# Query norms of a decoder layer moved from the gate stage to the mixer; memory norm moved into the second half of u

## The chip, the cores and the metric

The kernel runs on one core of a Trainium2 chip, in float32. The metric is the time of one execution on the device, in microseconds (us); three runs of the kernel before took 2217.03, 2217.82 and 2221.04 us, median 2217.82. A measurement is read together with the profile of one more execution.

TensorE does the matrix products, VectorE (DVE) and ScalarE (ACT) the elementwise work, GpSimd (POOL) a little of it, and SyncE (SP) issues the transfers. Float32 products are made from two-part numbers: each operand is split into a rounded part `hi` and a rest `lo`, and a product is three matmuls (hi hi, hi lo, lo hi). Every operand therefore costs one copy on ScalarE (the `hi`) and one subtract on VectorE (the `lo`) before TensorE can use it.

## The reference, cut to what matters

One layer: a half-step feed-forward block, a mixer with three branches, an output projection and a second feed-forward block. The change touches the combined projection and branches A and C.

```python
h = rmsnorm(x, mix_norm)                      # 1024 tokens x 1024 features
z = h @ w_in                                  # [u | v | c_q | c_kv | k_rope | q_mem | gate_A | gate_B | gate_C]
u, v = gelu(z_u), gelu(z_v)
y_a = u * (tril(W_s) layernorm(v) + b)        # over chunks of 128 tokens, 8 groups
y_b = latent attention of c_q, c_kv, k_rope   # untouched here
q  = rmsnorm(q_mem per head, mem_q_norm)      # 4 heads of 128
kv = rmsnorm(mem, mem_norm) @ mem_w_kv        # 256 memory tokens
y_c = softmax(q rmsnorm(k)^T / sqrt(128)) v
merged = sum_i sigmoid(gate_i + b_gate_i) * (y_i @ W_branch_i)
x = x + merged @ w_out
```

`rmsnorm(x, g)` is `x * rsqrt(mean(x*x) + 1e-6) * g`. The root of a query head is a number per token and head; it can be applied after the scores, and the kernel does so: queries go into the scores with their gain but without their root, and the softmax multiplies with the root.

## The kernel before, in words

**Stages, in order.** Feed-forward 1; the gates (`Gates`), which compute the three gate blocks and the four memory-query heads of z; the mixer (`mixer`), with the latent projections (`latent`, `qkv`), branch A (`sgu`), branch C (`mem_kv`, `mem_attention`), causal attention for branch B (`attention`); the output projection; feed-forward 2.

**The gates.** Two output blocks of 128 columns form a unit `f` (blocks `2f`, `2f+1`; units 0 to 11 are gates, 12 and 13 the four query heads). A unit is a Strassen scheme of seven half-sized products (`unit_steps`, 84 matmuls): weights come by DMA into `x4`/`w4` tiles, VectorE makes their sums (line 1295), and parts `a`, `s`, `t`, `l` are split into pairs of `wide` tiles (five pairs of them, lines 135 and 136). `emit` collects a block's two halves of 512 tokens in a `raw` tile (three of them in the whole kernel); a gate gets its sigmoid (line 1523) and is stored to memory.

A query block is treated otherwise in `emit`: `fold` squares its halves on ScalarE (line 1548, shown by the profile as line 1547), putting the two heads of a pair on partitions 0 to 63 and 64 to 127, and GpSimd adds the two foldings (line 1550); `split_gain` splits the whole block with its gain into a `wide` pair (lines 139 and 140), which is stored to `mq` (line 1537). `picked` (line 1558) sums the squares per token with 128x2 matmuls in the middle of the second next unit.

`Gates.run` (line 1561) fixes TensorE's order by hand: units 3, 4, 12, 13, 5, 6, ... 11. The other engines' order is made by a planner, which goes by program order and by its own estimate of when things are ready. In units 5 to 7 of that run `mem_norm` (line 700) loads the memory (1 MB), makes its root, scales it, splits it into `x4` tiles and stores the parts to `mrows`; it takes six `x4` tiles of ten, of which the weight loads want two or four a unit.

**Branch A, `sgu`.** No order is fixed by hand here: the planner orders all engines. v is made in two halves of 512 tokens, each eight feature tiles deep (96 matmuls a half, `gelu_rows`, lines 606 to 616), then gelu, layernorm on VectorE, split. Then u in two halves likewise; its weights `w_u` come in four chunks of two feature tiles, each through a `raw` tile (line 96) and a split into a `wide` pair (lines 130 and 131). After each half of u comes the spatial mixing. In the second half of u, `mem_rows` loads the stored memory rows into four `h4` tiles (line 733), and after its gelu a one-element exp (line 663) is issued whose only purpose is to bring ScalarE's exp table in; it reads a constant.

**Branch C.** `mem_kv` makes keys, then values, of the memory: three branch-A steps (`fill(3)`, 12 matmuls each), the key product, the key norm (`head_norm`), two more steps (`fill(2)`), the value product. `mem_attention` runs a list of scores (S), turns (T), values (V) and further branch-A steps (F), ten F in all; `scores` uses one of two double PSUM tiles (`mm`), which come free only when the softmax's exps (line 796) have read them.

## Time and profile before

The profiled execution took 2216.38 us; its span, from the first to the last instruction, is 2214.7 us.

| | |
|---|---|
| median of three runs | 2217.82 us |
| profiled execution, its span | 2216.38, 2214.7 us |
| TensorE busy, share of the span | 2183.5 us, 99% |
| VectorE, ScalarE, GpSimd busy | 1537.4, 904.4, 277.9 us |
| mean granted TensorE clock | 0.996 |
| the stages of the change | gates' hand-ordered units about 690 to 955 us; v and u about 1056 to 1150 us; memory products and attention about 1150 to 1260 us |

Busy time is the time in which an engine had an instruction under way. In a row of waits the first name is the waiting engine with the tile that it was to write and its line; the second is what released it. Idle time of an engine other than TensorE costs nothing here unless TensorE then waits for it. Lines are those of the kernel before.

### The profile page before, as it was taken

Reading aid. Unit: us, or ns where it says so; the run is one execution under the profiler, and the core shown is the slowest. Engines: PE = TensorE matmul, PEld = TensorE weight load, DVE = VectorE, ACT = ScalarE, POOL = GpSimd, SP = SyncE. Lnnn points to the kernel's source line nnn. Section 1 sums busy time; section 2 is a strip of 40 time slices with the busy share of each in tenths; the row PEclk is TensorE's granted clock in tenths of the full one; section 3 lists DMA queues with packets and bytes.
Section 4 is the critical chain, followed back from the end, with each engine's and each line's share of the span. In section 5 each row is a group of like instructions: output and inputs, shape, how many; then the busy total and the mean of one; then the engine's idle time right before and its main releaser. Section 6 shows DMA issues by size and latency. Waiting matters only on the chain.

```text
span 2214.7 us, 27600 instructions
## 1 busy us (share of the span) xinstructions
PE 2183.5 (99%) x10280; PEld 1820.2 (82%) x10280; DVE 1537.4 (69%) x2378; ACT 904.4 (41%) x1499; POOL 277.9 (13%) x269
## 2 busy tenths in 40 slices
PE   9999999999999989999999999999999999999999
PEld 5888888888887778889888889988888888888887
DVE  7966666589898456546845668885886666657884
ACT  6422222243455343344423448843342222224332
POOL 2012121100000000002201331140001121210000
PEclk9999999999999999999999999999999999999999
DMA  4242333484432333332554550075033333338543
GB/s 144 81 152 99 100 104 98 165 306 146 143 110 95 116 131 134 124 114 99 177 174 143 193 204 30 30 289 205 29 108 107 100 114 100 114 104 298 178 129 105
DMA packets 116087, 298.51 MB, mean 135 GB/s; under 512 B 13680, under 2 KB 22000, under 8 KB 115952
## 3 DMA queue, kind: packets, MB, share of 16 engines
q1 hardware_dynamic: 115952, 296.74, 39.1%
q8 instruction: 81, 1.33, 0.3%
q14 instruction: 54, 0.44, 0.1%
HBM read 208.09 MB, written 88.60 MB: 134 GB/s over the span
## 4 chain that ended last, share of the span: by engine, by line
PE 90%; DVE 5%; ACT 3%; DMA 1%; issue 1%; POOL 0%; ACTq 0%; SPq 0%; DVEq 0%; POOLq 0%
PE one L147 13%; PE one L148 13%; PE one L149 13%; PE bank L147 13%; PE bank L149 13%; PE bank L148 13%; PE mm L147 2%; PE mm L149 2%; PE mm L148 2%; PE bank L921 1%; PE bank L936 1%; PE bank L427 1%; PE bank L937 1%; DVE wlo L136 1%; DMA x<-in_w_gate_dram 1%
## 5 line engine op out<-in xcount | busy, mean ns | idle before, releaser
L135 ACT CAST whi<-x 128x1024 fp32r<-128x1024 f32 (+1 forms) x195 | 185.0, 953 | 474.9 <-PE one L148 199.4
L1322 DVE TENSOR_TENSOR t<-t,one 128x512 f32<-128x512 f32 x182 | 125.0, 687 | 234.2 <-PE one L149 234.1
L147 PE MATMUL bank<-h,whi 128*128 128x512 f32 x660 | 258.7, 392 | 8.4 <-ACT whi L135 8.4
L149 PE MATMUL bank<-h,wlo 128*128 128x512 f32 x660 | 258.4, 392 | 1.1 <-DVE wlo L136 1.1
L148 PE MATMUL bank<-h,whi 128*128 128x512 f32 x660 | 258.2, 391 | 0.0
L136 DVE TENSOR_TENSOR wlo<-x,whi 128x1024 fp32r<-128x1024 f32 (+1 forms) x195 | 232.7, 1197 | 30.8 <-ACT whi L135 30.5
L147 PE MATMUL one<-h,whi 128*128 128x512 f32 x492 | 192.9, 392 | 0.0
L148 PE MATMUL one<-h,whi 128*128 128x512 f32 x492 | 192.1, 391 | 0.0
L149 PE MATMUL one<-h,wlo 128*128 128x512 f32 x492 | 192.0, 390 | 0.0
L1765 POOL TENSOR_TENSOR raw<-raw 128x512 f32<-128x512 f32 x38 | 63.0, 1657 | 790.1 <-DVE raw L1620 790.1
L147 PE MATMUL one<-w,whi 128*128 128x512 f32 x408 | 159.3, 391 | 0.5 <-DVE t L1322 0.5
L149 PE MATMUL one<-w,wlo 128*128 128x512 f32 x408 | 158.8, 389 | 0.0
L148 PE MATMUL one<-w,whi 128*128 128x512 f32 x408 | 158.7, 389 | 0.0
L130 ACT CAST whi<-w 128x1024 fp32r<-128x1024 f32 (+1 forms) x108 | 95.1, 899 | 145.0 <-PE one L148 62.7
L147 PEld LDWEIGHTS bank<-h,whi 128*128 128x128 f32 x660 | 124.8, 189 | 34.9 <-ACT whi L135 9.2
L131 DVE TENSOR_TENSOR wlo<-w,whi 128x1024 fp32r<-128x1024 f32 (+1 forms) x108 | 110.2, 1034 | 61.0 <-ACT whi L130 60.9
L149 PEld LDWEIGHTS bank<-h,wlo 128*128 128x128 f32 x660 | 124.8, 189 | 28.0 <-DVE wlo L136 2.2
L148 PEld LDWEIGHTS bank<-h,whi 128*128 128x128 f32 x660 | 124.8, 189 | 25.9
L147 PE MATMUL bank<-whi 128*128 128x512 f32 x352 | 136.9, 389 | 0.0
L148 PE MATMUL bank<-wlo,whi 128*128 128x512 f32 x352 | 136.9, 389 | 0.0
L149 PE MATMUL bank<-whi,wlo 128*128 128x512 f32 x352 | 136.9, 389 | 0.0
L149 PEld LDWEIGHTS one<-h,wlo 128*128 128x128 f32 x492 | 92.8, 189 | 19.3
(378 smaller groups left out, 4970.8 us busy)
## 6 DMA issues: line engine op xcount, KB each, us to landing
x<-in_ffn_w_gu_dram SPq DMA_DIRECT2D x78, 512.0 KB, 5.2
w<-tdt SPq DMA_DIRECT2D x40, 512.0 KB, 4.6
tdb<-raw SPq DMA_DIRECT2D x64, 256.0 KB, 2.1
h<-in_ffn_w_down_dram SPq DMA_DIRECT2D x64, 256.0 KB, 6.0
w<-tdb SPq DMA_DIRECT2D x30, 512.0 KB, 4.7
tdt<-w SPq DMA_DIRECT2D x48, 256.0 KB, 2.1
gate<-raw SPq DMA_DIRECT2D x23, 512.0 KB, 2.6
tdt<-raw SPq DMA_DIRECT2D x40, 256.0 KB, 2.7
```

The lines of the kernel that those rows point to most:

```text
L130: self.nc.scalar.copy(hi, src)
L131: return (eng or self.nc.vector).tensor_tensor(lo, src, hi.bitcast(F32), op=ALU.subtract)
L135: self.nc.scalar.copy(hi, src)
L136: return lambda: self.nc.vector.tensor_tensor(lo, src, hi.bitcast(F32), op=ALU.subtract)
L147: i = mmul(out, s[0], m[0], start=first, stop=False, **kw)
L148: mmul(out, s[0], m[1], start=False, stop=False, **kw)
L149: self.last = mmul(out, s[1], m[0], start=False, stop=last, **kw)
L427: nc.tensor.transpose(b[:m, k * P:(k + 1) * P], s, self.ident)
L921: nc.tensor.transpose(b[:, at:at + P], prs[t][:, kk * P:(kk + 1) * P], self.ident)
L936: nc.tensor.matmul(o, w, pt[0], start=n == 0, stop=False)
L1322: return self.nc.vector.tensor_tensor(out, x, y, op=ALU.add)
L1765: sub = lambda d, x, y: (eng or nc.gpsimd).tensor_tensor(d, x, y, op=ALU.subtract)
```

## The change

1. The query blocks come apart from the sums of squares. A query block is stored to memory like a gate (`z`, 28 blocks instead of 24). Its gain split (`parts`) is put on a list, and each later unit takes one entry off it, behind its split of part t. Folding, picking and the roots leave the gates.
2. The order of units becomes 3, 4, 12, 5, 6, 13, 7, ... 11.
3. In `sgu`, ahead of w_u's load, `mem_root` loads the memory into two raw tiles and sums its squares, and `mem_query_roots` loads the query blocks back, for each pair of heads into two raw tiles, with head 0 of the pair on the lower and head 1 on the upper 64 partitions (eight loads of 256 KB), squares them in place and adds them on GpSimd. Two of these raw tiles stay in use until the picks.
4. The token sums of the memory and the picks of the queries run on TensorE ahead of the feature tiles 5 and 6 of u's first half; order-only edges tie the neighbours to them.
5. `mem_rows` no longer loads prepared rows: it loads the memory a second time and scales and splits it in u's second half. `mem_norm` and the `mrows` store are gone.
6. The one-element exp reads the last element of u's gelu instead of a constant.
7. `fill(2)` is gone from `mem_kv`; `mem_attention`'s list has three F more: after the second scores, after the first values and after the second values.

```diff
@@ -603,15 +603,19 @@
         for j in range(4):
             self.mm3(ps, wb[j], tuple(x[:, hf * 512:hf * 512 + 512] for x in yt[j]), j == 0, j == 3)
-    def gelu_rows(self, dst, h, w, pairs):
+    def gelu_rows(self, dst, h, w, pairs, amid={}):
         gelu = lambda d, x: self.nc.scalar.activation(d, x, ACT.Gelu)
         ps = [self.mm() for _ in range(2)] if pairs else [self.bank() for _ in range(4)]
         for d in range(DT):
+            then = amid[d]() if d in amid else None
             for i in range(4):
                 b = ps[i // 2][:, i % 2] if pairs else ps[i]
-                self.mm3(b, tuple(x[:, i * P:(i + 1) * P] for x in h[d]), w[d], d == 0, d == DT - 1)
+                first = self.mm3(b, tuple(x[:, i * P:(i + 1) * P] for x in h[d]), w[d], d == 0, d == DT - 1)
+                if then:
+                    self.after(first, then)
+                then = None
         for i, b in enumerate(ps):
             gelu(dst[:, 2 * i:2 * i + 2] if pairs else dst[:, i], b)
@@ -650,6 +654,9 @@
                         nc.vector.scalar_tensor_tensor(
                             v[:, k], in0=v[:, k], scalar=r[:, k:k + 1], in1=ln_b, op0=ALU.mult, op1=ALU.add)
                     self.split(vhi[:, i:i + 2], vlo[:, i:i + 2], v)
+            roots = self.mem_root(), self.mem_query_roots()
+            for x in roots:
+                next(x)
             w = self.load(a["w_u"])
             yt = [self.split_pair() for _ in range(4)]
             for hf in range(2):
@@ -658,9 +665,10 @@
                     mt = self.mem_rows()
                     branch = self.branches(0, yt, sink)
                     next(branch)
-                self.gelu_rows(u, h[hf], w, hf == 0)
+                self.gelu_rows(
+                    u, h[hf], w, hf == 0, {} if hf else {5 + n: lambda x=x: next(x) for n, x in enumerate(roots)})
                 if hf:
-                    nc.scalar.activation(self.stat("warm", 1), self.ones, ACT.Exp)
+                    nc.scalar.activation(self.stat("warm", 1), u[:, 3, SGW - 1:], ACT.Exp)
                     rooms = [v8(n).rearrange("p (a b) w -> p a (b w)", a=2) for n in ("v_hi", "v_lo")]
                     late = self.mem_queries(1, iter([tuple(x[:, i] for x in rooms) for i in range(2)]))
                     queries = self.mem_queries(0, iter(lambda: self.split_pair(self.h4), None)) + late
@@ -697,41 +705,66 @@
         x = x.rearrange("p t h d -> p (t h) d")
         nc.vector.tensor_tensor(x, x, r.unsqueeze(2).to_broadcast([P, nh, MD]), op=ALU.mult)
-    def mem_norm(self, kept):
-        nc, a = self.nc, self.a
-        x = [self.x4() for _ in range(2)]
-        for n, t in enumerate(x):
-            nc.sync.dma_start(
-                t.rearrange("p a (b m) -> p (a b) m", b=2), a["mem"][:, 4 * n:4 * n + 4])
+    def mem_root(self):
         acc = None
-        for n in range(4):
-            acc = self.norm_feed(acc, x[n // 2][:, n % 2], 512)
-        nc.vector.tensor_tensor(acc[:, :ML], acc[:, :ML], acc[:, ML:], op=ALU.add)
+        for n in range(2):
+            x = self.raw()
+            self.nc.sync.dma_start(
+                x.rearrange("p (c m) -> p c m", m=ML), self.a["mem"][:, 4 * n:4 * n + 4])
+            for i in range(2):
+                acc = self.norm_feed(acc, x[:, i * 512:i * 512 + 512], 512)
+        self.nc.vector.tensor_tensor(acc[:, :ML], acc[:, :ML], acc[:, ML:], op=ALU.add)
         yield
-        r = self.rms(self.token_sums(acc[:, :ML]), ML // P, D)
-        yield
-        scale = self.norm_scale(r)
-        for n, t in enumerate(x):
-            hi, lo = (self.x4(F32R) for _ in range(2))
-            for c in range(4):
-                at = slice(c % 2 * ML, c % 2 * ML + ML)
-                self.norm_put(
-                    hi[:, c // 2, at], lo[:, c // 2, at], t[:, c // 2, at],
-                    self.g_mem[:, 4 * n + c:4 * n + c + 1], scale)
-            for d, y in zip(kept[n], (hi, lo)):
-                nc.sync.dma_start(d, y.bitcast(F32))
+        r = self.m_r = self.const.tile([P, ML // P], F32, name="m_r")
+        ss = self.token_sums(acc[:, :ML], late=True)
+        last = self.final
+        self.nc.vector.tensor_copy(r, self.rms(ss, ML // P, D))
+        yield last
     def mem_rows(self):
         views = lambda ts: [t[:, i].rearrange("p (c m) -> p c m", m=ML)[:, c]
                             for t in ts for i in range(2) for c in range(2)]
-        hi, lo = ([self.h4(F32R) for _ in range(2)] for _ in range(2))
-        for n in range(2):
-            for t, src in zip((hi[n], lo[n]), self.mt[n]):
-                self.nc.sync.dma_start(t.bitcast(F32), src)
-        return views(hi), views(lo)
+        x4 = [self.h4() for _ in range(2)]
+        x, hi, lo = views(x4), *(views([self.h4(F32R) for _ in range(2)]) for _ in range(2))
+        for n, t in enumerate(x4):
+            self.nc.sync.dma_start(
+                t.rearrange("p a (b m) -> p (a b) m", b=2), self.a["mem"][:, 4 * n:4 * n + 4])
+        scale = self.norm_scale(self.m_r, late=True, bank=lambda: self.mm()[:, 0])
+        for c in range(DT):
+            self.norm_put(hi[c], lo[c], x[c], self.g_mem[:, c:c + 1], scale)
+        return hi, lo
+    def mem_query_roots(self):
+        nc = self.nc
+        sq = []
+        for pair in range(MH // 2):
+            ts = [self.raw() for _ in range(2)]
+            for n, t in enumerate(ts):
+                for o in range(2):
+                    src = self.z[ZQ + 2 * pair + o][n * P // 2:(n + 1) * P // 2]
+                    nc.sync.dma_start(t[o * P // 2:(o + 1) * P // 2], src.rearrange("p a w -> p (a w)"))
+                nc.scalar.activation(t, t, ACT.Square)
+            nc.gpsimd.tensor_tensor(ts[0], ts[0], ts[1], op=ALU.add)
+            sq.append(ts[0])
+        yield
+        b = self.bank()[:, :NT * MH]
+        for pair, x in enumerate(sq):
+            for t in range(NT):
+                at = t * MH + 2 * pair
+                i = nc.tensor.matmul(b[:, at:at + 2], x[:, t * P:(t + 1) * P], self.pick, start=True, stop=True)
+                if pair == t == 0:
+                    self.after(i, self.last)
+        self.mq_r = self.const.tile([P, NT * MH], F32, name="mq_r")
+        nc.vector.tensor_copy(self.mq_r, self.rms(b, NT * MH, MD))
+        self.mq_nr = self.const.tile([P, NT * MH], F32, name="mq_nr")
+        nc.gpsimd.tensor_scalar(self.mq_nr, self.mq_r, -1.0, None, op0=ALU.mult)
+        yield i
     def mem_kv(self, mt, fill):
@@ -753,7 +786,6 @@
         w = self.load(a["mem_w_kv"][1])
         x = self.h4().rearrange("p a (h d) -> p a h d", h=MH)
         self.head_norm(x, [ps[:, 0], ps[:, 1]])
-        fill(2)
         ps = product(w)
         for hh in range(0, MH, 2):
             self.to_feature(
@@ -825,9 +857,9 @@
         F = lambda: next(filler, None)
         yt = [self.split_pair(self.h4) for _ in range(MH)]
         for f, *x in (
-                (S, 0, 0), (F,), (S, 0, 1), (F,), (T, 0, 0), (S, 1, 0), (F,), (T, 0, 1), (S, 1, 1), (F,),
-                (V, 0), (T, 1, 0), (S, 2, 0), (F,), (T, 1, 1), (S, 2, 1), (F,), (V, 1), (T, 2, 0), (S, 3, 0), (F,),
-                (T, 2, 1), (S, 3, 1), (F,), (V, 2), (T, 3, 0), (F,), (T, 3, 1), (F,), (V, 3)):
+                (S, 0, 0), (F,), (S, 0, 1), (F,), (F,), (T, 0, 0), (S, 1, 0), (F,), (T, 0, 1), (S, 1, 1), (F,),
+                (V, 0), (F,), (T, 1, 0), (S, 2, 0), (F,), (T, 1, 1), (S, 2, 1), (F,), (V, 1), (F,), (T, 2, 0),
+                (S, 3, 0), (F,), (T, 2, 1), (S, 3, 1), (F,), (V, 2), (T, 3, 0), (F,), (T, 3, 1), (F,), (V, 3)):
             f(*x)
         for _ in filler:
             pass
@@ -1100,7 +1132,7 @@
                     (0, 1), {0: gates.w0[0], 1: {}}, ([(1, "t")], [(0, "a")]),
                     [lambda: None, do(gates.fetch, 2, [self.x4, gates.w4])], third=(2, [self.x4, gates.w4], ()))
             gates.run(x1d, r0)
-            self.sig, self.mq, self.mt = gates.z, gates.q, gates.m
+            self.sig, self.z, self.mq = gates.z, gates.z, gates.q
         with self.banks("mixps") as self.pm:
             merged = self.mixer(norm)
         with tc.tile_pool(name="f2", bufs=1) as fp, self.banks("f2ps") as self.pm:
@@ -1261,7 +1293,7 @@
     def __init__(self, k, w, pool, norm):
         self.k, self.nc, self.norm, self.w, self.pool = k, k.nc, norm, w, pool
-        self.quad, self.made, self.mark = {}, {}, None
+        self.quad, self.made, self.mark, self.extra = {}, {}, None, []
     def w4(self, dt=F32):
@@ -1351,6 +1383,8 @@
             w |= d
         else:
             w |= self.weights(f, "t")
+            if self.extra:
+                self.extra.pop(0)()
         self.product(a, w, "a12", "b21", False)
         self.emit(f, 0, 1, None, a)
         self.product(x, w, "s1", "t1", False)
@@ -1497,10 +1531,9 @@
     def __init__(self, k, w, pool, norm):
         super().__init__(k, w, pool, norm)
-        self.z = [k.dram.tile([P, 2, 512], F32, name=f"gate{i}") for i in range(ZQ)]
+        self.z = [k.dram.tile([P, 2, 512], F32, name=f"gate{i}") for i in range(ZB)]
         self.q = k.dram.tile([MH, 2, P, S], F32, name="mq")
-        self.m = k.dram.tile([2, 2, P, 2, 512], F32, name="mrows")
-        self.o, self.w0, self.folds = {}, {}, {}
+        self.o, self.w0 = {}, {}
     def first(self, f):
@@ -1524,39 +1557,19 @@
         elif row is None:
             self.nc.scalar.copy(d, ps)
         o[1] += 1
-        if n >= ZQ:
-            self.fold(n - ZQ, half, d)
         if o[1] == 2:
             t = self.o.pop(n)[0]
-            if n < ZQ:
-                self.nc.sync.dma_start(self.z[n], t)
-            else:
-                qs = k.wide("whi"), k.wide("wlo")
-                k.split_gain(*qs, t.rearrange("p a w -> p (a w)"), k.gq_m)
-                for x, q in zip(qs, self.q[n - ZQ]):
-                    self.nc.sync.dma_start(q, x.bitcast(F32))
-    def fold(self, head, half, d):
-        nc, o = self.nc, head % 2
-        first = (head // 2, half) not in self.folds
-        if first:
-            self.folds[head // 2, half] = [self.k.row() for _ in range(2)]
-        ts = self.folds[head // 2, half]
-        for i, t in enumerate(ts):
-            nc.scalar.activation(
-                t[o * P // 2:(o + 1) * P // 2], d[i * P // 2:(i + 1) * P // 2], ACT.Square)
-        if not first:
-            nc.gpsimd.tensor_tensor(ts[0], ts[0], ts[1], op=ALU.add)
-    def picked(self, pair, b):
-        for half in range(2):
-            sq = self.folds.pop((pair, half))[0]
-            for t in range(4):
-                at = (4 * half + t) * MH + 2 * pair
-                self.nc.tensor.matmul(
-                    b[:, at:at + 2], sq[:, t * P:(t + 1) * P], self.k.pick, start=True, stop=True)
+            self.nc.sync.dma_start(self.z[n], t)
+            if n >= ZQ:
+                self.extra.append(lambda: self.parts(n - ZQ, t))
+    def parts(self, head, t):
+        k = self.k
+        qs = k.wide("whi"), k.wide("wlo")
+        k.split_gain(*qs, t.rearrange("p a w -> p (a w)"), k.gq_m)
+        for x, q in zip(qs, self.q[head]):
+            self.nc.sync.dma_start(q, x.bitcast(F32))
     def run(self, x1d, r0):
@@ -1565,8 +1578,8 @@
         last, queries = ZQ // 2 - 1, (ZQ // 2, ZQ // 2 + 1)
         E = mybir.EngineType
         with k.tc.manual_schedule(engines={E.PE}):
-            for n, f in enumerate([3, 4, *queries, *range(5, last + 1)]):
-                self.fetch(f, [x4, w4, x4, w4] if n % 2 else [x4] * 4)
+            for n, f in enumerate([3, 4, queries[0], 5, 6, queries[1], *range(7, last + 1)]):
+                self.fetch(f, [x4] * 4 if n % 2 == 0 else [x4, w4, x4, w4])
                 if f == last:
                     k.w_cq = list(k.fetch(k.a["w_cq"], [x4, x4]))
                     for p in range(2):
@@ -1575,23 +1588,7 @@
                     norm.s[0] = k.norm_scale(r0)
                     for p in range(2):
                         norm.norm(0, p)
-                steps = self.unit_steps(f)
-                next(steps)
-                if n == 4:
-                    mem = k.mem_norm(self.m)
-                if 4 <= n < 7:
-                    next(mem, None)
-                if n in (3, 4):
-                    if n == 3:
-                        b = k.bank()
-                    self.picked(n - 3, b)
-                for _ in steps:
-                    pass
-                if n == 4:
-                    k.mq_r = k.const.tile([P, NT * MH], F32, name="mq_r")
-                    self.nc.vector.tensor_copy(k.mq_r, k.rms(b[:, :NT * MH], NT * MH, MD))
-                    k.mq_nr = k.const.tile([P, NT * MH], F32, name="mq_nr")
-                    self.nc.gpsimd.tensor_scalar(k.mq_nr, k.mq_r, -1.0, None, op0=ALU.mult)
+                self.unit(f)
             for p in range(2):
                 norm.put("b12", p, norm.t.t[0, p])
```

## The prediction

> **What bounds the kernel now.** I read the page first: busy time by engine.
>
> ```profile
> PE 2183.5 (99%) x10280; PEld 1820.2 (82%) x10280; DVE 1537.4 (69%) x2378; ACT 904.4 (41%) x1499; POOL 277.9 (13%) x269
> ```
>
> TensorE is busy in 2183.5 of 2214.7 us, and the change leaves its matmuls as many as they were (the picks, token sums and transposes only move). So all that can be won lies in some 31 us of idle time and in whatever slow stretches the idle time causes; the change has to be costed wait by wait. The view of waits, TensorE alone, whole run, says where the idle time is (total us, times, longest):
>
> ```profile
> PE bank L147 <- ACT whi L135: 8.4, 2, 4.2
> PE one L147 <- DVE raw L1322: 3.7, 4, 1.6
> PE mm L147 <- ACT v_hi L796: 3.5, 1, 3.5
> ```
>
> The first row is two equal waits of 4.2 us. The timeline puts the first at the end of a query unit (lines are start, length, instruction; idle time before it in brackets):
>
> ```profile
> 770.14 1.28 ACT L1547 ACTIVATE t<-raw 64x512 f32<-64x512 f32 x2 [1.45 <-DVE raw L1322]
> 771.44 1.15 ACT L139 ACTIVATE whi<-raw,gq_m 128x1024 fp32r<-128x1024 f32 x1
> ...
> 775.21 1.98 ACT L135 CAST whi<-x 128x1024 fp32r<-128x1024 f32 x2
> ...
> 775.33 1.28 DVE L140 SCALAR_TENSOR_TENSOR wlo<-raw,gq_m,whi 128x1024 fp32r<-128x1024 f32 x1 [1.31 <-ACT whi L139]
> ...
> 776.29 0.79 PE L147 MATMUL bank<-h,whi 128*128 128x512 f32 x1 [4.19 <-ACT whi L135]
> ...
> 778.82 0.63 PE L148 MATMUL bank<-h,whi 128*128 128x512 f32 x1
> ...
> 781.71 0.39 PE L149 MATMUL bank<-h,wlo 128*128 128x512 f32 x1
> ```
>
> ScalarE works off squares (L1547) and the gain split (L139), the rows shown and the same again for the second head, from 770.1 to 775.2 before it comes to the next unit's weight split (L135), and TensorE waits for that. Then its matmuls last 0.63 instead of 0.39 us until 781.7: the price of a wait is more than its idle time. So I price the stage by windows (length; PE busy us and matmuls; the other engines; granted clock):
>
> ```profile
> 690.00:740.00 50.00, 50.00 (x220) 41.02 (x221) 33.43 (x44) 21.92 (x29) 0.00 (x0) 1.00 0.44 148
> ...
> 761.70:778.40 16.70, 12.21 (x50) 9.27 (x49) 7.01 (x8) 10.63 (x15) 2.56 (x2) 0.89 0.31 124
> 778.40:789.90 11.50, 11.50 (x54) 9.65 (x53) 5.31 (x8) 1.33 (x3) 0.00 (x0) 0.86 0.33 105
> 789.90:806.60 16.70, 11.73 (x50) 9.10 (x49) 7.17 (x9) 10.59 (x15) 2.55 (x2) 0.97 0.29 119
> 806.60:821.20 14.60, 14.09 (x66) 11.51 (x65) 10.97 (x23) 5.99 (x10) 0.00 (x0) 0.92 0.48 153
> ...
> 855.00:870.00 15.00, 13.77 (x60) 10.92 (x59) 11.05 (x19) 6.41 (x9) 0.00 (x0) 1.00 0.75 261
> ```
> ```profile
> L1558 PE MATMUL bank<-pick,t x32: 165/251/251, 781.9 to 811.3; 128*128 128x2 f32 x32
> 782.10 1.68 PE bank L1558 x16
> ```
>
> Undisturbed, 220 matmuls take 50 us, 4.4 per us. From 761.7 to 821.2 (59.5 us) there are 220 too, 32 of them picks at 1.68 us for 16. The rest should take 188/4.4 = 42.7 us, with the picks' 3.4 that is 46.1: **13.4 us lost**. From 855 to 870 the 60 matmuls should take 13.6: **1.4 lost**. That one is the memory norm's: the chain there runs from its store through a weight load to DVE.
>
> ```profile
> 853.47 2.11 DMA mrows<-x
> ...
> 856.31 6.72 DMA x<-in_w_gate_dram
> ```
>
> **The change part by part.**
>
> *Gates.* Squares (8 ACT pairs of 1.27), POOL adds and picks leave the stage; so does the memory norm, and with it six x4 tiles, which are what the weight load at 856 waited for. Left are four gain splits, 1.15 ACT and 1.28 DVE each with two stores, one per later unit, behind that unit's t split. A unit has 84 matmuls, 19.1 us; in the undisturbed window ScalarE is busy 21.9 of 50 and VectorE 33.4 of 50, so a unit leaves 10.7 us of ACT and 6.3 of DVE idle: they cover 1.15 and 1.28. Without that cover four splits cost 4 x 2.43 = 9.7. The new hold is the raw tile: head 1's stays until the second unit after, where its split is issued just ahead of the sigmoid that needs a raw, and that unit's other raw is stored by then. Four more gate stores of 512 KB replace four mrows and are waited for by nobody until the mixer. Between a gain of 14.8 and 5.1 I take **-14.8**, for the windows of units without extras show no idle TensorE.
>
> *Exp table and fills.* The second place is the first softmax of memory attention:
>
> ```profile
> 0.81 1.28 ACT L663 ACT_TABLE_LOAD   x1 [0.81 <-PEq L2009]
> 1198.18 1.28 ACT L796 ACT_TABLE_LOAD   x1 [6.45 <-DVE m_mx L792]
> 1199.48 0.56 ACT L796 ACTIVATE v_hi<-mm,m_mx,mq_nr 128x256 f32<-128x256 f32 x1
> 1201.83 0.58 PE L147 MATMUL mm<-h,h 128*128 128x256 f32 x1 [3.51 <-ACT v_hi L796]
> 1202.20 0.42 PE L148 MATMUL mm<-h,h 128*128 128x256 f32 x1
> ...
> 1205.04 0.28 PE L147 MATMUL mm<-h,h 128*128 128x256 f32 x1
> ```
>
> The warm-up exp (L663) was hoisted to the program's start, where its table was replaced at once; the real load stands in the wait. Its price is 3.5 idle and 14 matmuls at about 0.21 instead of 0.12 us spacing, some 1.3 (0.42 falls to 0.28 us a piece only near 1205): 4.8. Tied to u's last gelu, the 1.28 load goes where ScalarE must then split weights for the memory product; uncovered it costs 1.28, and I take 0.7, half. The start wins nothing: there ScalarE still waits for x. The wait shrinks to 2.2, and a branch step (12 matmuls, 2.7 us) that now follows the second scores covers it. So I take **-4.8** of bounds -1.3 (table alone) and -4.8, and **+0.7**. The same moved steps face the small waits behind, 2.2 us in all:
>
> ```profile
> PE bank L148 <- DVE wlo L131: 0.7, 2, 0.5
> PE bank L147 <- DVE wlo L131: 0.6, 1, 0.6
> PE bank L839 <- DVE h L131: 0.5, 1, 0.5
> PE bank L147 <- DVE h L131: 0.4, 1, 0.4
> ```
>
> Of these I take **-1**, between 0 and -2.2. The two steps taken from between the memory products hid head_norm; the second product, 96 matmuls or some 11 us, hides it still.
>
> *Mixer, restacked loads.* Here the change adds waits. There are three raw tiles. In program order two memory loads and four pairs of restack loads now come before w_u's four chunks, and the two pair sums keep two raws until the picks ahead of feature tile 6 of u's first half. What stands now:
>
> ```profile
> 1061.85 1.75 SPq L96 DMA_DIRECT2D raw<-in_w_u_dram  x1
> ...
> 1068.52 2.79 SPq L96 DMA_DIRECT2D raw<-in_w_u_dram  x3
> L147 PE MATMUL mm<-whi,h x32: 389/389/389, 1099.7 to 1120.8; 128*128 128x512 f32 x32
> DMA to landing us min/median/max: 3.3/4.2/6.3
> L1550 POOL TENSOR_TENSOR t<-t x4: 1267/1276/1290, 771.5 to 802.4; 128x512 f32<-128x512 f32 x4
> 1078.38 0.74 POOL L363 TENSOR_TENSOR q<-rot,rot 128x256 f32<-128x256 f32 x1
> ```
>
> The landing row is that of raw tiles between 1050 and 1120. One raw's way: memory load from 1061.85 (up to 6.3, squares 1.3) to 1069.4; second restack pair (4.2 to 6.3, square 1.15) to about 1076; its add, 2 x 1.28, only after POOL's rotations at 1079.1, so 1081.7; fourth pair and its add, 4.2 to 6.3 + 1.15 + 2.55, so 1089.6 to 1091.7. Only then w_u's first chunk, through the one free raw: 4.2 and some 1.9 of splitting, 1096 to 1098. TensorE wants it at 1099.7, and a new chunk every 5.45 us; one raw gives one every 6.1. Chunk four is ready near 1116, wanted at 1118. So it just fits, if VectorE is prompt, and it is not idle:
>
> ```profile
> L644 DVE BATCH_NORM_STATS2 bn<-u 128x6 f32<-128x512 f32 x8 | 5.1, 675 | 9.8 <-ACT u L609 9.8
> ```
>
> From 1083 to 1121 its only idle stretch is the 9.8 us before the first layernorm; w_u's splits move from there into it. Queued behind a late chunk on TensorE is all of u. Bounds: 0, and one half's layernorm ahead, about 12. I take **+2**.
>
> The Trainium skill, "SBUF — State Buffer", section "Can I just issue two DMAs to hit both halves?", speaks against the restacking: two transfers to the two halves of the partitions run after one another, each over half the ports (196 GB/s there). By it, as an estimate, a pair needs some 1.5 us more than one full load, three in a row 4.5, the added wait is about 5 instead of 2, and the sum comes out 3 us higher. No 64-partition load of this size stands in the trace before.
>
> *Memory norm in u's second half.* Two loads replace four (the queue is no fuller); then 8 VectorE scalings, 8 ACT copies and 8 subtracts:
>
> ```profile
> L130 ACT CAST x<-x 128x256 fp32r<-128x256 f32 x8 | 3.1, 407 | 0.2 <-DVE x L411 0.2
> L131 DVE TENSOR_TENSOR x<-x,x 128x256 fp32r<-128x256 f32 x8 | 2.8, 419 | 0.0
> ```
>
> That is some 7 us of VectorE under 22 us of u matmuls, done before the memory product: 0; 7 if that cover fails.
>
> Sum: -14.8 - 4.8 + 0.7 - 1 + 2 = -17.9. The profiled execution took 2216.38 (span 2214.7 and 1.7 around it), the median of the runs is 1.44 above: 2217.82 - 17.9 = **2199.9**.
>
> **Rivals.**
>
> *The raw shortage bites:* splits queue behind layernorm, w_u is 6 to 14 late, say 10 for 2: 2208. For it: the arithmetic above leaves 2 us. Against it: v's two halves were run interleaved when a chunk was late, and u's could be.
>
> *The splits still stop the units:* with one per unit they wait in front of the next unit's split, gates win 5.1: 2210. Against it: their inputs lie ready a unit ahead.
>
> *Slower:* the restack chain is so late that w_u's first chunk comes after 1120, 20 us behind its want; from there the loss at u eats the whole gain of 19.9. With each pair at twice 6.3 and the adds held off until v's layernorm of the first half is through, near 1099.7, the second pair's add ends at 1102, the fourth's at 1118.5, the chunk is split at 1124.6, 25 late, and the next three add 2: 2217.8 - 19.9 + 27 = 2225. Against it: nothing in the chain needs VectorE, and no raw load there took over 6.3.
>
> *Everything fits:* no new wait, all small ones gone: 2217.82 - 14.8 - 4.8 - 2.2 = 2196, a bit less if windows hide more.
>
> **How the numbers follow.** Chances: forecast 0.55 (its own range 2196 to 2205), shortage 0.22, splits 0.09, slower 0.07, all fits 0.07. A measurement of this kernel can tell about 0.2%, 4.4 us. Shortage and splits lie at the edge of that in their bad halves, so faster 0.88, same 0.06, slower 0.06. The range, 2194 to 2211, holds the forecast, all that fits and most of the shortage.
>
> **What would show it.** The two 4.2 us waits for L135 and the 0.63 us matmuls behind query units must be gone, and TensorE without idle time from 690 to 940; the exp table load must stand behind u's last gelu, and the wait for L796 fall under 1 us. A new wait of TensorE for the split of w_u, or for the picks, is the shortage. I am wrong if the units after a query unit wait for L139, or if u starts more than 5 us after v's last matmul.

## The result, and the profile after

The changed kernel takes **2205.8 us** (median of four runs, 2205.3 to 2206.2) against 2219.4 us for the kernel before on the same chip (2217.0 to 2221.0); the ratio is 0.9939, 95% interval 0.9922 to 0.9957. Faster, by 13.6 us, where 17.9 were forecast; the time is 5.9 us above the forecast and inside its range. The profiled execution took 2205.72 us, its span 2204.0.

Where the 13.6 us came from is read best from windows whose ends are the same instructions in both kernels: the table load at the start of the gate stage, the mixer's first matmul, the first spatial mixing behind u's first half, the last transpose of u, the first transpose of causal attention, the end. First the kernel before (length; TensorE, its weight loads, VectorE, ScalarE, GpSimd busy; granted clock; DMA share; GB/s), then the one after:

```profile
683.74:962.05 278.31, 265.54 (x1167) 217.12 (x1166) 163.58 (x241) 118.39 (x166) 5.42 (x5) 0.98 0.38 134
962.05:1121.45 159.40, 158.11 (x825) 139.59 (x824) 100.09 (x246) 65.70 (x153) 28.86 (x37) 1.00 0.39 128
1121.45:1163.85 42.40, 42.10 (x223) 35.90 (x222) 18.71 (x36) 14.56 (x26) 0.00 (x0) 1.00 0.50 162
1163.85:1302.19 138.34, 132.70 (x702) 113.64 (x701) 74.03 (x139) 50.84 (x138) 37.49 (x29) 0.99 0.55 200
1302.19:2214.70 912.51, 906.51 (x4429) 764.08 (x4427) 660.22 (x994) 388.07 (x652) 125.36 (x141) 1.00 0.37 126
```
```profile
686.18:943.50 257.32, 255.76 (x1130) 210.92 (x1129) 153.71 (x200) 103.51 (x138) 0.00 (x0) 1.00 0.41 140
943.50:1112.38 168.88, 165.23 (x861) 144.49 (x860) 109.27 (x272) 71.99 (x161) 34.80 (x40) 0.99 0.39 125
1112.38:1159.17 46.79, 43.87 (x225) 37.26 (x224) 24.44 (x52) 18.36 (x36) 0.00 (x0) 0.96 0.54 183
1159.17:1291.48 132.31, 130.76 (x702) 112.15 (x701) 77.09 (x139) 50.41 (x137) 37.98 (x29) 1.00 0.57 208
1291.48:2204.00 912.52, 906.42 (x4429) 763.86 (x4427) 660.62 (x994) 388.03 (x652) 125.25 (x141) 1.00 0.37 126
```

Stage by stage the change is -21.0, +9.5, +4.4, -6.0 and 0.0 us: -13.1, which is the difference of the medians but for 0.5. Ahead of the first window the profiled execution after is 2.4 us *later* (686.18 against 683.74); that is scatter of the first transfers (shown by the first experiment below), and it is why the spans differ by 10.7 us only and the windows by 13.1. About 3.9 us of picks and token sums moved from the first window to the second (32 picks 3.4; four matmuls of sums 0.5: a variant below whose second window holds the sums and no picks is 159.88 long, 0.48 more than before). Without them the gates gave **17.1**, and v with u's first half took back **5.6**, u's second half **4.4**.

TensorE's waits of the whole run after, the ones that answer to those shown of before (total us, times, longest; the third row is the first weight transfer of the run), and the stretch that held the two 4.2 us waits:

```profile
PE bank L147 <- DVE x L131: 4.0, 2, 2.7
PE mm L147 <- ACT whi L130: 1.7, 1, 1.7
PE bank L1670 <- DMA w<-in_ffn_w_gu_dram: 1.5, 1, 1.5
```
```profile
764.10:823.60 59.50, 59.50 (x265) 49.25 (x264) 34.87 (x44) 22.16 (x29) 0.00 (x0) 1.00 0.39 134
```

265 matmuls now fill the 59.5 us in which the same view of the kernel before (761.70 to 821.20) has 214 at a clock of 0.91; both waits are gone. In their place stand two new ones in the sgu stage. The timeline of the changed kernel shows them (start, length, engine, line, instruction, idle time before it):

```profile
1074.34 2.40 POOL L753 TENSOR_TENSOR raw<-raw 128x1024 f32<-128x1024 f32 x1 [8.76 <-ACT raw L752]
...
1074.97 2.32 DVE L652 SCALAR_TENSOR_TENSOR u<-u,mv,ln_g 128x512 f32<-128x512 f32 x1
...
1076.76 14.62 SPq L96 DMA_DIRECT2D raw<-in_w_u_dram  x3
...
1081.24 0.69 DVE L131 TENSOR_TENSOR wlo<-raw,whi 128x512 fp32r<-128x512 f32 x1
...
1084.50 0.68 DVE L131 TENSOR_TENSOR wlo<-raw,whi 128x512 fp32r<-128x512 f32 x1
...
1089.02 1.14 ACT L130 CAST whi<-raw 128x512 fp32r<-128x512 f32 x2 [0.88 <-DMA raw<-in_w_u_dram]
...
1089.69 0.49 PE L147 MATMUL mm<-whi,h 128*128 128x512 f32 x1 [1.66 <-ACT whi L130]
...
1116.78 3.21 DVE L411 SCALAR_TENSOR_TENSOR h<-h,c_mem_norm,mm 128x256 f32<-128x256 f32 x8
1119.91 1.28 DVE L131 TENSOR_TENSOR x<-bank,x 128x512 fp32r<-128x512 f32 x2
1120.65 0.50 PE L147 MATMUL bank<-whi,h 128*128 128x512 f32 x1 [2.71 <-DVE x L131]
```

The first is the raw shortage: w_u's first chunk is asked for at 1076.76, when the second GpSimd add has freed a raw tile. The one free tile then has to be split before chunk two can be fetched; VectorE's second subtract comes only at 1084.50, 3.3 us after the first, because layernorm lies between them, so the chunk lands late and TensorE waits 1.66 us for it. The second was not foreseen: the eight scalings of the memory norm (L411) stand on VectorE ahead of the subtracts that empty the banks of u's transposes, and u's second half waits 2.71 us for a bank. Behind each come matmuls of 0.63 us.

The signs named for the exp table came true: the load stands behind u's last gelu, and the wait at the first softmax, 3.5 us before, is 0.3 (the timeline, then the waits from 1180 to 1200):

```profile
1145.99 1.28 ACT L671 ACT_TABLE_LOAD   x1
```
```profile
PE mm L147 <- ACT v_hi L828: 0.3, 1, 0.3
```

### The profile page after: what moved, and what is told of

It reads as the page before. It is cut to its first block, busy times and chain, and to the rows that moved or that the text cites. A ratio compares the mean times of both kernels' runs of the same rounds, so it can differ in the third digit from the quotient of the medians.

```text
span 2204.0 us, 27591 instructions
## 1 busy us (share of the span) xinstructions
PE 2181.8 (99%) x10280; PEld 1819.7 (83%) x10280; DVE 1545.2 (70%) x2379; ACT 897.6 (41%) x1486; POOL 279.6 (13%) x267
## 4 chain that ended last, share of the span: by engine, by line
PE 89%; DVE 5%; ACT 2%; DMA 2%; POOL 1%; issue 1%; SPq 0%; ACTq 0%; POOLq 0%; DVEq 0%
PE one L147 14%; PE one L148 14%; PE one L149 14%; PE bank L147 13%; PE bank L149 13%; PE bank L148 13%; PE mm L147 2%; PE mm L148 2%; PE mm L149 2%; PE bank L953 1%; DMA w<-in_ffn_w_gu_dram 1%; PE bank L968 1%; PE bank L969 1%; PE bank L427 1%; POOL t L1199 1%
## 5 line engine op out<-in xcount | busy, mean ns | idle before, releaser
L135 ACT CAST whi<-x 128x1024 fp32r<-128x1024 f32 (+1 forms) x195 | 185.5, 953 | 484.1 <-PE one L148 206.4
L131 DVE TENSOR_TENSOR wlo<-w,whi 128x1024 fp32r<-128x1024 f32 (+1 forms) x108 | 110.2, 1035 | 60.4 <-ACT whi L130 60.3
```

What stands on the lines that cost most here:

```text
L131: return (eng or self.nc.vector).tensor_tensor(lo, src, hi.bitcast(F32), op=ALU.subtract)
L135: self.nc.scalar.copy(hi, src)
```

## The experiments

All are variants of the changed kernel; e3's edit is taken up in e4, e4's in e8, and so on to e9 and e11, the others stand alone. Differences are to the 2205.66 us of e1. The variants ran in groups on different chips, where the kernel before had medians of 2217.1 to 2218.8 us; a difference of one or two us between the medians of different groups (e1 to e4; e5 to e8; e9 and e10; e11) is therefore not to be read, and the windows decide.

**e1: the changed kernel again.**

> The changed kernel as it is, beside which the variants are read. Theory: 2205.8 us again, with the loss of the sgu stage in the same two places: about 5.4 us in u's first half (the late second chunk of w_u and the slow matmuls after it) and about 4.6 us at the start of u's second half (the wait for a bank held by a subtract of the transposes and the slow matmuls after it). The first wait of TensorE for a weight transfer at 8.4 us, which the kernel before did not have in its profiled execution, should come or go by itself if it is scatter of the first transfers; if it is the change's, it stands at 1.5 us again.

2205.66 us (2204.05 to 2206.6). Both losses stand where they stood, 1.63 and 2.71 us of waiting; the stage windows are 257.32, 169.11, 46.82 and 132.37 us. The wait for the first weight transfer is gone and the gate stage starts at 684.16 instead of 686.18: scatter. The kernel before scatters as well, 2215.0 to 2223.0 us over all its runs here, so the windows are the sharper measure.

**e2: memory norm behind the transposes' subtracts** (one order on VectorE, nothing else; `done` is the last subtract of the first half's transposes).

```diff
-            self.norm_put(hi[c], lo[c], x[c], self.g_mem[:, c:c + 1], scale)
+            i = self.norm_put(hi[c], lo[c], x[c], self.g_mem[:, c:c + 1], scale)
+            if c == 0:
+                self.after(i, done)
```

> Only an order on VectorE is added: the first of the eight memory scalings comes behind the last subtract of the first half's transposes. Theory: the 2.7 us wait for DVE x L131 and the 0.63 us matmuls behind it vanish, 4.6 us, so 2201.2 us. Rival: the memory rows are then late for the memory product, or the bank was held by something else; then the time stays at 2205.8 us or a wait of some us stands at the memory product.

2201.92 us, -3.7. The window of u's second half:

```profile
1112.95:1155.54 42.59, 42.30 (x225) 36.10 (x223) 24.52 (x52) 19.09 (x36) 0.00 (x0) 1.00 0.56 187
```

42.59 instead of 46.82: the wait and the slow matmuls are gone, 4.2 us, and no wait has come at the memory product. The norm's work is free there; its place in VectorE's queue was not. (The window ahead of it was 3.0 us longer in this execution: the picks and 12 matmuls behind them were slow, where the repeat has eight slow ones behind its wait for w_u, and the idle time was 0.9 us more. Of such stretches more below.)

**e3: w_u ahead of the restacked loads, picks in u's second half** (and, in a line not shown, into a tile `mm` instead of a bank).

```diff
-            for x in roots:
-                next(x)
+            next(roots[0])
             w = self.load(a["w_u"])
+            next(roots[1])
...
-  {} if hf else {5 + n: lambda x=x: next(x) for n, x in enumerate(roots)}
+  {5 + hf: lambda x=roots[hf]: next(x)}
```

> The loads of w_u are issued ahead of the restacked loads, and the picks go into u's second half (into an mm tile). Theory: the shortage of raw tiles is what makes w_u late, so the waits for whi and wlo between 1081 and 1095 us vanish, 5.4 us, so 2200.4 us. Rival: the shortage moves on to the branch weights or the picks, or the chunks are late because VectorE works off the layernorm first; then 2204 us or more, with a new wait behind u or the same waits for wlo.

2204.53 us, only -1.1. The waits for w_u are gone, as the theory had it, and the window up to the spatial mixing is 159.91 us. But two waits stand right behind, in the view of waits from 1080 to 1120:

```profile
PE bank L147 <- DVE u L679: 3.1, 1, 3.1
PE bank L147 <- DVE rms_v L176: 2.4, 1, 2.4
```

That is the rival, a new wait behind u. The shortage had hidden the next limit, VectorE's work on v. For the 3.1 us: u's gelu needs the single tile `u`, and v's layernorm holds that until its last subtract. For the 2.4 us: a bank holds the memory's token sums until VectorE reads them (L176, at 1105.71), and it does so only between v's last two subtracts.

**e4: both edits.**

> Both edits together. Theory: the two losses are separate and add up: 2205.8 - 4.6 - 5.4 = 2195.8 us, below both kernels. Rival: what one edit wins the other loses (the squares, picks and scalings then all lie in u's second half): 2200 us.

2203.78 us: the gains do not add up, and the time is above even the rival's 2200. The bank wait behind the transposes is gone (second half's window 54.71 instead of 56.69 in the variant before), the two waits for VectorE stand at 1.9 and 3.1 us.

**e8: restacked loads and branch weights later in the program's order.**

```diff
-            next(roots[1])
...
                     mt = self.mem_rows(done)
+                    next(roots[1])
                     branch = self.branches(0, yt, sink)
-                    next(branch)
...
                 if hf:
+                    next(branch)
                     nc.scalar.activation(self.stat("warm", 1), u[:, 3, SGW - 1:], ACT.Exp)
```

> e4 with two more moves in the program's order: the restacked loads and squares come behind u's first half, the branch weights' load and split behind the matmuls of u's second half. Theory: in e4 u's first half ended with waits of 1.9 and 3.1 us because u has one tile, which v's layernorm held until 1107, and VectorE lost about 3.4 us of that to the branch weights' split (1.3) and a 2.3 us instruction beside a GpSimd add (2.1). With both out of the way the two waits shrink by about 3.4 us, and the slow matmuls behind them go: 2203.8 - 3.5 to 4.5, so 2199.3 to 2200.3. Rival: the picks or the branch weights are then late in u's second half or behind it; then 2203.8 us or more, with a wait there.

2203.97 us, no gain over the variant before, and the timeline says why:

```profile
1092.29 2.50 POOL L756 TENSOR_TENSOR raw<-raw 128x1024 f32<-128x1024 f32 x1 [5.96 <-ACT raw L755]
...
1092.55 2.27 DVE L176 TENSOR_SCALAR rms_v<-mv 128x2 f32<-128x2 f32 x1
...
1099.89 1.28 DVE L131 TENSOR_TENSOR wlo<-raw,whi 128x512 fp32r<-128x512 f32 x2
...
1103.62 1.21 DVE L131 TENSOR_TENSOR v_lo<-u,v_hi 128x1024 fp32r<-128x1024 f32 x1
...
1104.93 1.94 ACT L610 ACTIVATE u<-mm 128x1024 f32<-128x1024 f32 x2 [1.35 <-DVE rs_y L158]
...
1107.44 0.58 PE L147 MATMUL bank<-v_hi,x 128*128 128x256 f32 x1 [3.06 <-DVE u L680]
```

The planner fetched and split the branch weights (L131 at 1099.89) and made the add (L756) as early as before; a change of program order that the planner undoes is no experiment. The chain itself is plain here: last subtract of v, gelu of u (its releaser is given as L158, the instruction right behind that subtract), u's product, and only then TensorE. In it stand the branch split and an instruction on two numbers a partition that took 2.27 us beside the GpSimd add (0.13 and 0.16 without one, in the next variant).

**e9: the squares held by an order** (`cast` is ScalarE's last copy of the first half's transposes). The picks move as well, from ahead of feature tile 6 to ahead of tile 7 of u's second half, counted from 0.

```diff
-                nc.scalar.activation(t, t, ACT.Square)
+                i = nc.scalar.activation(t, t, ACT.Square)
+                if pair == n == 0:
+                    self.after(i, self.cast)
...
-  {5 + hf: lambda x=roots[hf]: next(x)}
+  {5 + 2 * hf: lambda x=roots[hf]: next(x)}
```

> e8 once more, but now forced: the first square of the restacked rows is ordered behind the last cast of the first half's transposes, so that the first GpSimd add, the second pair's loads and the branch weights' load and split all come behind u's first half. In e8 the planner had put them where e4 has them, VectorE's order was the same, and so was the time. Theory: VectorE is 3.4 us earlier through v's layernorm, u's tile is free 3.4 us earlier, and the two waits at the end of u's first half (1.5 and 3.1 us in e8) fall to 1 to 1.5 us together: 2203.9 - 3.4 and, with the slow matmuls that follow a wait, down to -5: 2198.9 to 2200.5. Rival: VectorE's layernorm is not what the waits are for, or the picks and the branch weights come late in u's second half; then 2203 us or more.

2197.51 us, -8.2; ratio to the kernel before 0.9909 (0.9897 to 0.9922). v's last subtract now comes 4.7 us earlier (1098.93 instead of 1103.62), and of the two waits 0.2 us is left; 3.4 us and a rest of 1 to 1.5 were expected. The other 1.3 us lie further ahead: in e8 the first GpSimd add stood beside the subtracts of v's first half, and the two took 4.29 us; without it they take 2.36, and v's second gelu starts 1.5 us earlier (1087.18 instead of 1088.64). The windows from the gate stage to causal attention are together 6.8 us shorter than the repeat's. u's second half still holds a slow stretch, though no idle time of over 0.3 us stands between 997 and 1134 us:

```profile
1125.88 3.63 PE L766 MATMUL mm<-pick,raw 128*128 128x2 f32 x32
...
1130.98 0.63 PE L149 MATMUL bank<-whi,h 128*128 128x512 f32 x1
...
1133.12 0.62 PE L148 MATMUL bank<-wlo,h 128*128 128x512 f32 x1
```

**e11: the picks in two runs of 16.**

```diff
-  {5 + 2 * hf: lambda x=roots[hf]: next(x)}
+  {d: lambda x=roots[hf]: next(x) for d in ((5, 7) if hf else (5,))}
...
+            if pair == 0:
+                yield i
```

> e9 with its 32 picks in two runs of 16, the first ahead of u's sixth feature tile and the second ahead of its eighth, instead of all 32 in one run of 3.4 us. In e9 no idle time of over 0.3 us stands between 997 and 1134 us, and yet eight matmuls of 0.63 us follow the picks, 1.7 us. Theory: the long run of matmuls with two columns counts as idleness for the clock; in two runs of 1.7 us the slow matmuls vanish: 2197.5 - 1.7, so 2195.8 us. Rival: the slow stretch has another cause, and stays at the end of u's second half: 2197.5 us.

**2194.22 us** (2193.88 to 2194.77), ratio to the kernel before 0.9895 (0.9878 to 0.9911): the best version, 11.4 us below the changed kernel (9.8 by the windows). The windows from the mixer's first matmul to u's last transpose, and the picks:

```profile
941.24:1101.12 159.88, 158.59 (x829) 140.02 (x828) 104.31 (x256) 68.64 (x157) 30.02 (x37) 1.00 0.37 119
1101.12:1148.29 47.17, 46.87 (x260) 40.38 (x259) 28.30 (x69) 22.31 (x41) 5.08 (x3) 1.00 0.67 227
```
```profile
1120.55 1.84 PE L766 MATMUL mm<-pick,raw 128*128 128x2 f32 x16
...
1127.84 1.84 PE L766 MATMUL mm<-pick,raw 128*128 128x2 f32 x16
```

The clock is 1.00, no matmul of 0.63 us is left in u's second half, and the half is 2.3 us shorter than the 49.43 of the variant before. The slow matmuls were some 1.6 of that; the rest is two short waits for a weight's split behind them (0.54 and 0.23 us), which went as well. The median fell by 3.3 us where 1.7 were expected; what lies outside this half was not separated. What is left of idle time in both windows is 1.6 us, 1.29 of them in the latent stage as before.

**e10: full loads instead of halves.**

```diff
-                for o in range(2):
-                    src = self.z[ZQ + 2 * pair + o][n * P // 2:(n + 1) * P // 2]
-                    nc.sync.dma_start(t[o * P // 2:(o + 1) * P // 2], src.rearrange("p a w -> p (a w)"))
+                nc.sync.dma_start(t, self.z[ZQ + 2 * pair + n].rearrange("p a w -> p (a w)"))
```

> The changed kernel with each pair of 64-partition loads put together to one 128-partition load of the same 512 KB. The tiles then hold two whole heads' rows instead of restacked halves, so the sums of the query norm are of other rows; everything else is computed as before. Theory of the rule on two halves: a pair costs 1.5 us more than one full load, three in a row 4.5, so w_u's first two chunks come up to 4.5 us earlier and most of the 5.3 us lost in u's first half is saved: 2201 to 2203 us. Rival: the pair lands as one load does, and the second chunk waits for a raw tile that VectorE frees late in any case: 2205 to 2206 us, with the same wait of 1.6 us for whi in u's first half.

2201.94 us (2198.7 to 2205.9), -3.7. The timeline of this kernel:

```profile
1072.39 14.93 SPq L96 DMA_DIRECT2D raw<-in_w_u_dram  x3
...
1085.63 0.49 PE L147 MATMUL mm<-whi,h 128*128 128x512 f32 x1 [0.35 <-ACT whi L130]
```

Measured from the mixer's first matmul (942.07 here, 943.50 after), w_u's first chunk is asked for 2.9 us earlier, and the second chunk's wait is 0.35 instead of 1.66 us. So the restacking itself lengthens the chain by 2.9 us. The window up to the spatial mixing is 1.6 us shorter than in the repeat of the changed kernel (167.50 to 169.11). Another 1.6 are a slow stretch behind the 2.7 us wait that came in the repeat and not here, though the wait is the same; that the edit took it away is not shown. The six runs lie 7.2 us apart, so of the 3.7 only the first 1.6 can be put down to the full loads.

**e7: gain splits at once.**

```diff
-                self.extra.append(lambda: self.parts(n - ZQ, t))
+                self.parts(n - ZQ, t)
```

> The gain splits of a query unit's two heads are issued as its rows come out, not one per later unit; squares and picks stay out of the stage. Theory of the forecast's rival: the splits stop the next unit, 2.43 us each for four heads, 9.7 us, so up to 2215.4 us, with waits of TensorE for whi of L136 of some 2.4 us and more behind the two query units. Rival: it was the squares that stopped the units, two splits fit under a unit's 10.7 us of idle ScalarE, and the time stays at 2205.7 us.

2219.17 us; against the kernel before 1.0001 (0.9992 to 1.0009). The whole gain is gone, more than the 9.7 us of the theory. Timeline behind the first query unit, and the window of the stage:

```profile
773.85 1.15 ACT L139 ACTIVATE whi<-raw,gq_m 128x1024 fp32r<-128x1024 f32 x1 [1.95 <-DVE raw L1354]
774.91 1.98 ACT L135 CAST whi<-x 128x1024 fp32r<-128x1024 f32 x2
...
775.99 0.80 PE L147 MATMUL bank<-h,whi 128*128 128x512 f32 x1 [3.34 <-ACT whi L135]
```
```profile
684.28:955.80 271.52, 262.48 (x1129) 214.46 (x1128) 153.20 (x200) 103.49 (x138) 0.00 (x0) 0.97 0.39 133
```

The stage is 14.2 us longer than with the splits deferred (257.32): 7.5 of it idle (9.04 less the 1.56 idle there), the rest slow matmuls. ScalarE is idle 1.95 us ahead of the second head's split: that split waits for the unit's last rows, and the next unit's weights (L135), whose two loads were issued at 756 and landed within 6.4 us, stand behind it in the queue.

**e5: exp untied; e6: old fills.** The one puts the constant back into the warm-up exp; the other puts back the old list of branch steps and the two between the memory products.

> The warm-up exp reads the constant ones again, all else as changed. Theory by the prediction's terms: the table load moves to the program's start and a real one of 1.28 us stands ahead of the first softmax; TensorE's wait there grows from 0.27 to about 1.5 us, and up to 0.7 us comes back behind u: 2205.7 + 0.6 to 1.3, so 2206.3 to 2207. Rival: the branch steps that now lie there cover the load whole, and the tie was worth nothing: 2205.0 to 2205.7 us.

> The branch steps stand where the kernel before had them (two between the memory products, one fewer each at three places of memory attention), the tie stays. Theory by the prediction's terms: the wait at the first memory product behind the first softmax is 2.2 us again, with slow matmuls 3.5 us, and the small waits for 1 us: 2205.7 + 3.5 to 4.5, so 2209.2 to 2210.2. Rival: the tie alone took the wait away, and the fills are worth no more than 1 us: 2206.7 us.

2206.53 us (+0.9) and 2209.91 us (+4.3): each as by the prediction's terms. The runs of the first overlap those of e1, and its window up to causal attention (133.65 instead of 132.37 us) is the surer sign; the profiled execution of the second is the longest of its five, 2211.7 us, with 138.32 in that window. TensorE's waits, of the first and of the second:

```profile
PE mm L147 <- ACT v_hi L828: 1.3, 2, 0.8
```
```profile
PE mm L147 <- ACT v_hi L829: 2.3, 1, 2.3
PE bank L147 <- DVE wlo L131: 2.0, 1, 2.0
```

In the changed kernel the first of these is 0.3 us. The second wait of the old fills, 2.0 us for a branch weight, is one that the prediction did not have.

## Why the prediction was right or wrong

**The bound** was read rightly: TensorE's matmuls stayed as many, and every term of the result is its idle or slow time.

**Gates, forecast -14.8: right, 17.1 measured.** The two waits of 4.2 us and the slow matmuls behind them are gone, as named, and TensorE has no idle time from 692.5 to 943.5. Some 1.4 of the 2.3 us won beyond the forecast are a miscount: the prediction's four windows add up to 220 matmuls because those that lie across a border count twice; one window over the stretch has 214. That one split per unit hides was the step on which the rival (5.1) turned: with the splits at once the stage is 14.2 us longer, so the deferral carries most of the gain. Squares, adds, picks and memory norm are what is left, some 3 of 17 us; with the squares gone and the splits in place the waits were still 3.3 us each, not 4.2. The prediction's rows showed both squares and split ahead of the weights; the splits alone bring nearly the whole loss back. What the squares alone would cost was not run.

**Exp table and fills, forecast -4.8 + 0.7 - 1 = -5.1: right, -6.0.** The two runs split it: untied +0.9, old fills +4.3 where 3.5 to 4.5 were to come back. The +0.7 for the load behind u's gelu was not paid: u's second half is 46.82 us with it and, untied, without it, while the window up to causal attention grows from 132.37 to 133.65 us untied, by one load.

**Raw shortage, forecast +2, bounds 0 to 12: the first of two steps that failed.** 5.6 us measured. The chain was followed rightly, from the memory loads over two adds to the one free tile; four things in it were not.

First, restacked loads were costed at 4.2 to 6.3 us, while the changed kernel's transfers from 1040 to 1100 show

```profile
raw<-gate SPq DMA_DIRECT2D x8, 256.0 KB, 7.1
raw<-in_mem_dram SPq DMA_DIRECT2D x2, 512.0 KB, 6.5
```

and full loads take 2.9 us off the chain. The halves alone are not the 7.1: full loads took 5.8 at the same place, and the same halves 3.9 where they come later, behind w_u (e3). Second, the order on ScalarE and VectorE, here of the changed kernel:

```profile
1070.08 1.28 ACT L609 ACT_TABLE_LOAD   x1 [1.24 <-DMA raw<-gate]
1071.37 1.94 ACT L609 ACTIVATE u<-mm 128x1024 f32<-128x1024 f32 x2
1072.43 1.29 DVE L648 BATCH_NORM_STATS2 bn<-u 128x6 f32<-128x512 f32 x2 [11.13 <-ACT u L609]
1073.20 1.06 ACT L752 ACTIVATE raw<-raw 128x1024 f32<-128x1024 f32 x1
```

The prediction let the last square follow its rows at once. They had landed by 1070.1, but the square (L752) stood behind v's table load and gelus and ran 3.1 us later; in the kernel with full loads the gap is as long (1065.7 to 1068.84). Third, "if VectorE is prompt" did not hold: chunk two came 8.5 us behind chunk one (1081.2 to 1089.7), not 6.1. The prediction put w_u's splits into VectorE's idle stretch ahead of the first layernorm. That was misread: the 9.8 us ended at 1085.4 in the kernel before, and most of them lay ahead of 1083; in the changed kernel the stretch ended at 1072.4, and the first chunk's subtract came 8.8 us later, in the midst of layernorm. Fourth, the term priced a wait and no slow matmuls. TensorE's idle time in the window grew by 2.4 us (3.65 less 1.29), close to the 2; eight matmuls of 0.63 us lose 1.6 more, and the other 1.6 were not separated.

The Trainium skill, "SBUF — State Buffer", section "Can I just issue two DMAs to hit both halves?", says that two half-height transfers serialize; the estimate from it was 4.5 us for three pairs and an added wait of about 5 where the rows gave 2. The chain's 2.9 us is two thirds of that estimate. That the 5.6 us lost come near its 5 is luck: with full loads 4.2 of them stay (167.50 less 159.40 and the 3.9 that moved).

The rival of the shortage (2208) was nearer to the time than the forecast, which is luck as well: its price of 10 was nearly twice the 5.6, and the memory norm's loss, which it did not have, came on top. What the prediction did not see at all: had w_u come in time, the wait would only have moved, since VectorE's work on v holds the one `u` tile and a bank; e9 shows it by taking VectorE's other work out of the way.

**Memory norm in u's second half, forecast 0, "7 if that cover fails": the second step that failed, 4.4, of which 4.2 go with one order edge.** The cover did not fail: the memory product never waits. The cost lay ahead of it. The step asked when the norm's results are due, and not what stands behind the norm's instructions on VectorE: the subtracts that free the banks.

**The sum.** -17.1 - 6.0 + 5.6 + 4.4 = -13.1. The losses were 8.0 us more than forecast; that the time still fell within the range owes something to luck, the 3.2 us that gates and fills gave beyond their terms. With both losses undone the best variant is at 2194.2 us, below the 2196 of "everything fits". The case of a slower kernel was far: the first chunk was split 138 us into the mixer (1081.2 less 943.5), not 158 (1120 less 962.1). Of the signs named ahead, the new wait for w_u's split was the shortage, and u started at once behind v; the bank wait was on no list.

## What to carry to other kernels

Work that is moved under a cover is paid for at the head of its queue, not at its deadline: for each moved instruction ask what stands behind it on its engine, above all what frees a PSUM bank or a tile of a small ring. Four splits of 1.15 us, two behind each of two units, cost 14 us when they stood ahead of the next unit's weights, and left TensorE without idle time when each came with a later unit. And when a starved load is cured, look for the single-buffered tile that holds the same place next; prefer an order edge, for a planner may undo a mere change of program order.

## What was not expected of the hardware

**A run of narrow matmuls can slow the clock as idle time does.** Behind the 32 picks in one run (3.6 us, two columns each, no idle time) eight matmuls took 0.63 us instead of 0.39; with 16 and 16 none did. Of eleven profiled executions with one run of 32 in the mixer, eight show such a stretch within 1.5 us of its end, 6 to 12 matmuls that lose 0.2 us each, so 1.2 to 2.4 us; in the other three, the changed kernel's two among them, none follows. The Trainium skill, "TensorE: Matmul & The Clock Gate", section "Part 1: The HAM clock gate", ties the clock to how busy the array was in free-running windows of some 3.4 us; a run of picks of that length fits such a window, and the free-running window would also let a 2.7 us wait be followed by slow matmuls in one execution and not in another, as here. Why three had none is open; they are the three in which the 2.7 us wait a good 10 us later was followed by slow matmuls, while in the three others with that wait (old fills, full loads, splits at once) the picks had them and the wait did not.

**A GpSimd add holds up VectorE on the smallest operand.** Beside it a `tensor_scalar` on 128x2 took 2.27 us instead of 0.13, and a 128x512 product 2.32 instead of 0.74. The Trainium skill, "SBUF — State Buffer", section "Who interferes with whom", has an exclusive lock on a shared port between the two; the rows agree, and an add of 2.4 to 2.5 us cost VectorE 1.6 to 2.1 us here.
